# Storing the cumulative sums by chunk, joining small transfers, and starting the SSD and gate loads on GpSimd's queue

## The chip, the cores and the metric

The kernel runs on one core of one Trainium2 chip. Its time is the device time of one execution in microseconds (us). Before the change it is 2260.72 us (median of 3 runs, 2260.71 to 2261.99). A profiled execution is a run of its own: its own time was 2257.6 us, and its trace spans 2255.6 us from the first to the last instruction.

Engines are named as in the profile: PE is the matrix engine (TensorE), DVE is VectorE, ACT is ScalarE, POOL is GpSimd, SP is SyncE. SP does no arithmetic here; it starts transfers.

## The reference

One decoder layer in FP32, with 1024 tokens and a width of 1024. Cut to what matters here:

```python
h = rms_norm(x, norm_mix_g)
z, xbc, dt_raw, q_a, kv_a, k_rope, gates = split(h @ w_in)
# Mamba-2: y_t = sum_{s<=t} (C_t.B_s) exp(sum_{s<k<=t} a_k) x_s dt_s, in chunks of 128 tokens
#   a_cum = cumsum(dt * A) in each chunk; 4 groups of 8 heads
y_ssd = rms_norm_by_group((ssd(silu(conv4(xbc)), dt, a_cum) + d_skip*xs) * silu(z)) @ w_ssd_proj
y_mla = causal_attention(q, k, v) @ w_mla_proj          # 16 heads
g_ssd, g_mla = split(sigmoid(gates + gate_b))
x = x + (g_ssd * y_ssd + g_mla * y_mla) @ w_o
u_gate, u_val = split(conv3(rms_norm(x, norm_ffn_g) @ w_up))
x = x + (silu(u_gate) * u_val) @ w_down                 # d_ff 2816
```

## The kernel before

**Arithmetic.** Every FP32 product is made of three reduced-precision products. A matrix is split into a high part (`whi`, an ACT copy, L152) and a low part (`wlo`, a subtraction, L153), and `mm3` adds hi·hi, hi·lo and lo·hi (L174, L175, L176). The subtraction for weights runs on POOL until L1102 and on DVE after it (`w_eng`). A weight piece of 512 columns is loaded into `wraw`, which has two buffers, so one load runs while the piece before it is split; `whi` and `wlo` are double-buffered too.

**Stages.** (1) The first norm and the small projections, to about 118 us. (2) Attention, to about 700 us, with tiles of z and of the gates computed in its background. (3) The state-space part (SSD), 700 to about 1290 us: four groups g of eight heads, eight chunks of 128 tokens in each. In its background run the convolutions and z tiles of the next group and, in group 3, the output projection of attention (`mla_tiles`, from about 1140 us). (4) The merge, 1303 to 1570 us, in two halves of 512 tokens: for each 128 output channels `ct` a product with `w_ssd_proj`, then gate and sum, then the product with `w_o` and the residual x. (5) The gated MLP.

**What passes through DRAM.** The cumulative sums `ac_d` ([32 heads, 1024 tokens]), z (`z_d`), the gates (`g_d`), the attention output (`at_d`) with its denominators (`l_d`), SSD's output (`y_d`), the gated attention part (`m_d`) and the new residual (`x2_d`, called `x_d` in the profile) are stored and loaded again.

- In each SSD chunk, `abc_load` (L788) reads the chunk's 8 x 128 sums and repeats them on all 128 partitions, 512 KB, and `z_load` (L796) reads the chunk's z, 256 KB. Both are started by ACT. `abc` has three buffers, and the MLA tiles and loads borrow them in group 3; `zt` has two.
- In `mla_tiles`, `one` (L1028) loads the gate of one tile, 256 KB, on SP, placed directly behind the SP instruction ahead of it in program order, and stores the product in `m_d` (L1035).
- In the merge, the gate `gt` (L1213) and the attention part `mt` (L1215) of each `ct` are started by ACT, 16 of each. DVE makes `gt` times the product (L1223) and adds `mt` (L1224). The first weights of the MLP, `ur` (L1126, L1127), are four loads of 512 KB, started by SP in the second half's first steps of the program text.
- The residual x is loaded at L1237 in four transfers of 512 KB per half, and the sum of half 0 is stored in `x2_d` in four transfers of 512 KB (L1276), each before one norm. That norm (`norm`, L233 to L254) overwrites the same tile in place, so its last instruction (L254) waits for the store. The sum of half 1 is stored in 16 transfers of 128 KB on ACT (L1270).

**Order.** PE's order is written out: a chain of dependences (L1563 on) keeps its instructions in program order. On the other engines a scheduler sets the order when the program is built. Each engine and each queue then works strictly in that order, so an instruction that waits holds back all behind it on its engine. Where `behind(name)` stands, the instruction just written is tied behind another one.

## Time and profile before

| what | value |
|---|---|
| median of 3 runs | 2260.72 us |
| profiled execution, its own time | 2257.6 us |
| span of its trace | 2255.6 us |
| PE busy | 2184.2 us (97%) |
| DVE busy | 1433.8 us (64%) |
| ACT busy | 1010.7 us (45%) |
| POOL busy | 758.7 us (34%) |
| packets on SP's queue (q1) | 101232, 214.73 MB |
| packets on ACT's queue (q10) | 57520, 36.84 MB |

How it is read: a time of the trace is counted from its first instruction. "Waits" are groups of idle times, each with the engine that waited, its line, and what came last. A window gives the busy time of each engine, the TensorE clock that was granted, the mean busy share of the 16 DMA engines and what they moved. The share of the DMA engines is the time their packets took, which depends on the packets' size as well as on the bytes.

### The profile page before, as it was taken

To read this page: it belongs to the slowest core of one execution; us is meant where nothing else is said; L and a number is where in the kernel's file an instruction comes from. 1 tells how busy PE (TensorE), PEld (TensorE's weight loads), DVE (VectorE), ACT (ScalarE), POOL (GpSimd) and SP (SyncE) were. 2 spreads that over 40 slices of the span, in tenths; PEclk is the share of its full clock that TensorE was granted. 3 is DMA by queue.
4 is the path that set the end of the run, shared out by engine and by line. 5 is a ranking of instruction groups with operands and counts; after the bars stand their busy time and mean duration, and the time that the engine had idled before them with its cause. 6 is when DMAs were issued, how large, how long until landed. Compare 5 with 4: busy or idle time off the path is not lost.

```text
span 2255.6 us, 31367 instructions
## 1 busy us (share of the span) xinstructions
PE 2184.2 (97%) x11488; PEld 1771.6 (79%) x11488; DVE 1433.8 (64%) x2496; ACT 1010.7 (45%) x1852; POOL 758.7 (34%) x799
## 2 busy tenths in 40 slices
PE   8999999999999999999989999999899999999999
PEld 7877777777777887777877778989778888888887
DVE  4567665667662469897966845546887767774432
ACT  5444454454443446555644424325544444443231
POOL 2244433444232235464523300003365555510000
PEclk9999999999999999999999999999999999999999
DMA  4121111111114235654367556453122222237541
GB/s 144 58 67 49 49 43 53 54 53 38 53 49 121 67 89 143 174 153 153 107 176 218 181 198 227 159 168 113 56 94 79 80 84 78 81 124 259 198 138 66
DMA packets 158905, 253.56 MB, mean 112 GB/s; under 512 B 13504, under 2 KB 68480, under 8 KB 158752
## 3 DMA queue, kind: packets, MB, share of 16 engines
q1 hardware_dynamic: 101232, 214.73, 28.2%
q10 hardware_dynamic: 57520, 36.84, 6.9%
q8 instruction: 90, 1.47, 0.3%
q14 instruction: 63, 0.52, 0.1%
HBM read 194.63 MB, written 56.89 MB: 112 GB/s over the span
## 4 chain that ended last, share of the span: by engine, by line
PE 70%; DVE 16%; DMA 5%; ACT 4%; issue 2%; POOL 1%; SPq 0%; ACTq 0%; DVEq 0%; POOLq 0%
PE lin L174 11%; PE lin L176 11%; PE lin L175 11%; PE dps L174 8%; PE dps L176 8%; PE dps L175 8%; PE pv L669 2%; DMA rb<-at_d 2%; PE s L174 1%; DVE xg L812 1%; PE s L175 1%; PE s L176 1%; PE s L626 1%; DMA wraw<-in_w_mla 1%; DVE qk L587 1%
## 5 line engine op out<-in xcount | busy, mean ns | idle before, releaser
L174 PE MATMUL lin<-h,whi 128*128 128x512 f32 x1440 | 595.4, 413 | 10.8 <-DVE lt L329 7.9
L176 PE MATMUL lin<-h,wlo 128*128 128x512 f32 x1440 | 567.4, 394 | 9.4 <-DVE wlo L153 8.2
L175 PE MATMUL lin<-h,whi 128*128 128x512 f32 x1440 | 565.8, 393 | 0.0
L174 PEld LDWEIGHTS lin<-h,whi 128*128 128x128 f32 x1440 | 273.1, 190 | 94.2 <-issue 33.7
L176 PEld LDWEIGHTS lin<-h,wlo 128*128 128x128 f32 x1440 | 272.5, 189 | 71.3 <-DVE wlo L153 9.0
L175 PEld LDWEIGHTS lin<-h,whi 128*128 128x128 f32 x1440 | 273.6, 190 | 53.3 <-issue 6.7
L152 ACT CAST whi<-wraw 128x512 fp32r<-128x512 f32 x276 | 165.2, 618 | 268.8 <-PE lin L175 110.9
L153 POOL TENSOR_TENSOR wlo<-wraw,whi 128x512 fp32r<-128x512 f32 x134 | 196.1, 1481 | 232.7 <-ACT whi L152 215.8
L658 ACT ACTIVATE e<-s 128x512 f32<-128x512 f32 (+1 forms) x192 | 93.7, 492 | 166.0 <-DVE s L656 141.3
L663 POOL TENSOR_TENSOR acc<-acc,e 128x512 f32<-128x512 f32 (+3 forms) x80 | 79.6, 994 | 232.5 <-ACT e L658 219.0
L153 DVE TENSOR_TENSOR wlo<-wraw,whi 128x512 fp32r<-128x512 f32 x142 | 99.8, 721 | 87.1 <-ACT whi L152 86.8
L153 DVE TENSOR_TENSOR h<-ar,h 128x1024 fp32r<-128x1024 f32 x40 | 48.9, 1225 | 109.3 <-ACT h L152 109.1
L152 ACT CAST h<-ar 128x1024 fp32r<-128x1024 f32 x40 | 42.2, 1054 | 125.8 <-PE lin L175 115.0
L175 PE MATMUL dps<-wlo,h 128*128 128x512 f32 x240 | 93.4, 389 | 0.0
L174 PE MATMUL dps<-whi,h 128*128 128x512 f32 x240 | 93.4, 389 | 0.0
L176 PE MATMUL dps<-whi,h 128*128 128x512 f32 x240 | 93.4, 389 | 0.0
L850 ACT ACTIVATE seg<-abc,acum 128x128 f32<-128x128 f32 x256 | 82.0, 391 | 24.8 <-PE yp L891 16.7
L812 DVE SCALAR_TENSOR_TENSOR xg<-craw,cl,xg 128x1024 f32<-128x1024 f32 x48 | 75.9, 1580 | 18.2 <-ACT xg L810 17.8
L1191 POOL TENSOR_TENSOR h<-x,h 128x512 fp32r<-128x512 f32 x8 | 11.1, 1389 | 220.9 <-ACT h L1190 220.9
L663 DVE TENSOR_TENSOR acc<-acc,e 128x512 f32<-128x512 f32 (+3 forms) x80 | 53.5, 669 | 41.3 <-ACT e L658 40.7
L1138 ACT CAST xhi<-ur 128x512 fp32r<-128x512 f32 (+1 forms) x41 | 34.1, 831 | 88.9 <-PE dps L175 80.0
L669 PE MATMUL pv<-e,vt 128*64 128x512 f32 (+3 forms) x384 | 72.9, 498 | 0.0
(581 smaller groups left out, 5179.5 us busy)
## 6 DMA issues: line engine op xcount, KB each, us to landing
wraw<-in_w_main SPq DMA_DIRECT2D x112, 256.0 KB
ur<-in_w_up SPq DMA_DIRECT2D x44, 512.0 KB
ar<-a_d SPq DMA_DIRECT2D x40, 512.0 KB
abc<-ac_d ACTq DMA_DIRECT2D x32, 512.0 KB
wraw<-in_w_ssd SPq DMA_DIRECT2D x64, 256.0 KB
wraw<-in_w_down SPq DMA_DIRECT2D x44, 256.0 KB
a_d<-uc SPq DMA_DIRECT2D x22, 512.0 KB
g_d<-lt SPq DMA_DIRECT2D x32, 256.0 KB
```

The lines of the kernel that those rows point to most:

```text
L152: S.copy(hi, raw)
L153: (eng or V).tensor_sub(lo, raw, hi.bitcast(F32))
L174: PE.matmul(ps, lhsT=ah, rhs=bh, start=first, stop=False, **more)
L175: PE.matmul(ps, lhsT=ah, rhs=bl, start=False, stop=False, **more)
L176: PE.matmul(ps, lhsT=al, rhs=bh, start=False, stop=last, **more)
L587: V.tensor_tensor(qk[:, :, 2 + hd, 0:64], qk[:, :, 2 + hd, 0:64], rr[:, :, 2 + hd:3 + hd].broadcast_to([P, 4, 64]), op=ALU.mult)
L658: S.activation(e[:, c0:512], ps[:, 0:w], AF.Exp)
L663: (V if hd else G).tensor_tensor(accs[hd][:, c0:512], accs[hd][:, c0:512], e[:, c0:512], op=ALU.add)
L669: PE.matmul(pv[hd * 64:(hd + 1) * 64, c0:512], lhsT=vt[:, j, hd * 64:(hd + 1) * 64], rhs=es[hd][:, c0:512], start=first, stop=last)
L812: V.scalar_tensor_tensor(c, raw[:, k:k + T], col(cw + k), c, op0=ALU.mult, op1=ALU.add)
L850: S.activation(seg[:, hd, :], abc[:, hd, :], AF.Relu, bias=acum[:, c, 8 * g + hd:8 * g + hd + 1], scale=-1.0)
L1138: S.copy(hi, r)
```

## The change

```diff
-    ac_d = dram.tile([HEADS, T], F32, name="ac_d")
+    ac_d = dram.tile([NT, HEADS, P], F32, name="ac_d")
-    l_d = dram.tile([MH, T], F32, name="l_d")
+    l_d = dram.tile([4 * MH, 256], F32, name="l_d")
...
-    nc.sync.dma_start(out=ac_d, in_=act_)
+    nc.sync.dma_start(out=ac_d.rearrange("c h t -> h c t"), in_=act_.rearrange("h (c t) -> h c t", t=P))
...
-            for c in range(4):
-                a = half * 512 + (c % 2) * 256
-                nc.sync.dma_start(out=l_d[2 * pr + c // 2, a:a + 256], in_=lr[32 * c:32 * c + 1, 0:256])
+            r0 = 4 * (2 * pr + half)
+            nc.sync.dma_start(out=l_d[r0:r0 + 4, :], in_=lr[0:128:32, 0:256])
...
-                nc.scalar.dma_start(out=t, in_=ac_d[8 * g:8 * g + 8, c * P:(c + 1) * P].partition_broadcast(P))
+                nc.gpsimd.dma_start(out=t, in_=ac_d[c, 8 * g:8 * g + 8, :].partition_broadcast(P))
...
-                nc.scalar.dma_start(out=t, in_=z_d[4 * g * P:4 * (g + 1) * P, c * P:(c + 1) * P]
+                nc.gpsimd.dma_start(out=t, in_=z_d[4 * g * P:4 * (g + 1) * P, c * P:(c + 1) * P]
...
-                        name = last(mybir.EngineType.SP)
-                        nc.sync.dma_start(out=gt, in_=g_d[(8 + ct) * P:(9 + ct) * P, s])
-                        behind(name)
+                        nc.gpsimd.dma_start(out=gt, in_=g_d[(8 + ct) * P:(9 + ct) * P, s])
...
-    def w_raw(q):
+    def w_raw(q, name=None):
...
-        nc.sync.dma_start(out=q.r1, in_=w_up[q.j])
-        nc.sync.dma_start(out=q.r2, in_=w_up[FFT + q.j])
+        for raw, j in ((q.r1, q.j), (q.r2, FFT + q.j)):
+            nc.sync.dma_start(out=raw, in_=w_up[j])
+            if name:
+                behind(name)
...
-                    w_raw(q0)
-                    w_raw(q1)
+                    w_raw(q0, loaded)
+                    w_raw(q1, loaded)
...
-                    nc.scalar.dma_start(out=gt, in_=g_d[ct * P:(ct + 1) * P, s])
+                    nc.gpsimd.dma_start(out=gt, in_=g_d[ct * P:(ct + 1) * P, s])
-                    nc.scalar.dma_start(out=mt, in_=m_d[ct * P:(ct + 1) * P, s])
+                    nc.gpsimd.dma_start(out=mt, in_=m_d[ct * P:(ct + 1) * P, s])
...
-                for i in range(4):
-                    r0 = (half * 4 + i) * P
-                    nc.sync.dma_start(out=big[:, i, :], in_=x[r0:r0 + P, :])
-                    behind(loaded)
+                nc.sync.dma_start(out=big, in_=x[s, :].rearrange("(i p) c -> p i c", p=P))
+                behind(loaded)
...
-                                if half:
-                                    nc.scalar.dma_start(out=x2_d[512 + i * P:512 + (i + 1) * P, qs], in_=big[:, i, qs])
+                                if half and i == 3:
+                                    nc.scalar.dma_start(out=x2_d[s, qs].rearrange("(i p) c -> p i c", p=P),
+                                                        in_=big[:, :, qs])
...
-                    for i in range(4):
-                        nc.sync.dma_start(out=x2_d[i * P:(i + 1) * P, :], in_=big[:, i, :])
+                    nc.sync.dma_start(out=x2_d[s, :].rearrange("(i p) c -> p i c", p=P), in_=big)
```

`loaded` is the last weight load of step ct = 5 of the merge's half. The x load of each half stands behind it, before and after; in the changed program the `ur` loads stand behind that of half 0. The reads of `l_d` (L991 and L1066 before) follow its new shape. Counted over the program: SP starts 710 transfers instead of 783, ACT has 112 instructions fewer, and POOL has 112 more: 32 loads of `abc`, 32 of `zt`, 16 gates of `mla_tiles`, and 32 of `gt` and `mt`. PE's order is the same. Lines of the changed kernel are numbered one or two higher from L88 on.

Where the change moves instructions, three places matter below. The first is POOL in the SSD stage, one chunk, before (its `sq` stands at 959.7 us in the trace): `st` is the decay of the carried state, `sq` and `sqs` sum squares for the group norm, `rb` scales an attention tile, `wlo` are low parts of weights.

```order
L879 TENSOR_TENSOR st<-st,cdec 128x512 [waits DVE_49,PE_49]
L915 TENSOR_TENSOR sq__9571<-sq__9571 128x256 [waits Activation_49]
L916 TENSOR_TENSOR sqs<-sq__9571 128x128 [waits Pool_49]
L981 TENSOR_TENSOR rb<-rb,nb 128x512 [waits DMAHW6_49,DMAHW4_49,DMAHW3_49]
L153 TENSOR_TENSOR wlo<-wraw,whi 128x512 [waits DMAHW0_49,PE_49,Activation_49]
L153 TENSOR_TENSOR wlo<-wraw,whi 128x512 [waits DMAHW1_49,Activation_49]
```

The same place in the changed program:

```order
L879 TENSOR_TENSOR st<-st,cdec 128x512 [waits DVE_49,PE_49]
L788 DMA abc<-ac_d 128x1024 [waits DMASW3_49]
L796 DMA zt<-z_d 128x4x128 [waits DMASW4_49,DMASW0_49,DVE_49]
L915 TENSOR_TENSOR sq__9787<-sq__9787 128x256 [waits Activation_49]
L916 TENSOR_TENSOR sqs<-sq__9787 128x128 [waits Pool_49]
L981 TENSOR_TENSOR rb<-rb,nb 128x512 [waits DMAHW3_49,DMAHW5_49,DMAHW2_49,DMAHW1_49]
L154 TENSOR_TENSOR wlo<-wraw,whi 128x512 [waits DMAHW0_49,PE_49,Activation_49]
L154 TENSOR_TENSOR wlo<-wraw,whi 128x512 [waits DMAHW2_49,Activation_49]
```

The two loads now stand between the state decay and the group norm, ahead of the low parts.

The second place is POOL in group 3 of the changed program, with the gate loads of `mla_tiles` (L1029 there) among the low parts of its weights:

```order
L796 DMA zt<-z_d 128x4x128 [waits DMAHW1_49,DMASW6_49,DMAHW3_49,DMASW5_49,DVE_49]
L916 TENSOR_TENSOR sqs<-sq__11378 128x128 [waits Pool_49]
L1029 DMA rb<-g_d 128x512 [waits DMAHW4_49,DVE_49]
L154 TENSOR_TENSOR wlo<-wraw,whi 128x512 [waits PE_49,Activation_49]
L788 DMA abc<-ac_d 128x1024 [waits PE_49]
L154 TENSOR_TENSOR wlo<-wraw,whi 128x512 [waits DMAHW2_49,Activation_49]
L1029 DMA rb<-g_d 128x512 [waits DMAHW2_49,DMASW0_49,DVE_49]
```

Before, the gate loads and their waits stood on SP, the sums' and z's on ACT.

The third place is DVE at the end of half 0 of the merge. Before, with the four stores of the new residual (`x_13408` is its tile, L254 the norm that overwrites it):

```order
L1266 TENSOR_TENSOR x_13408<-dps,x_13408 128x256 [waits PE_49]
L248 SCALAR_TENSOR_TENSOR nst<-nst 128x1 [waits DVE_49]
L254 TENSOR_SCALAR x_13408<-x_13408,nst 128x1024 [waits DMAHW0_49]
L153 TENSOR_TENSOR wlo<-wraw,whi 128x512 [waits DMAHW6_49,Activation_49]
L153 TENSOR_TENSOR wlo<-wraw,whi 128x512 [waits DMAHW7_49,Activation_49]
```

And in the changed program, with one store:

```order
L154 TENSOR_TENSOR wlo<-wraw,whi 128x512 [waits DMAHW0_49,Activation_49]
L255 TENSOR_SCALAR x_13360<-x_13360,nst 128x1024 [waits DMAHW1_49]
L255 TENSOR_SCALAR x_13360<-x_13360,nst 128x1024 [waits DVE_49]
L234 TENSOR_REDUCE nst<-sq_13362 128x1 [waits DVE_49] x2
L154 TENSOR_TENSOR wlo<-wraw,whi 128x512 [waits DMAHW2_49,PE_49,Activation_49]
L242 TENSOR_SCALAR nst<-nst 128x1 [waits DVE_49] x2
L154 TENSOR_TENSOR wlo<-wraw,whi 128x512 [waits DMAHW3_49,Activation_49]
```

The norm's wait is now for the only store, and two low parts that the next output tile needs stand behind it.

More of the change, by code (lines that the diff above doesn't have):

```diff
@@ L989, in normalize @@
                 for hd in range(2):
-                    nc.sync.dma_start(out=rb[64 * hd:64 * hd + 64, :], in_=l_d[2 * k + hd, s].partition_broadcast(64))
+                    r0 = 4 * (2 * k + n % 2) + 2 * hd
+                    nc.sync.dma_start(out=rb[64 * hd:64 * hd + 64, :],
+                                      in_=l_d[r0:r0 + 2, :].rearrange("a b -> (a b)").partition_broadcast(64))
                 loaded.append((raw, rb, at_d[k * P:(k + 1) * P, s]))
@@ L1065, in tile_hybrid_layer @@
         ls = dp.tile([P, P], F32, name="bt")
-        lv = l_d.rearrange("h (c t) -> (h c) t", t=P)
+        lv = l_d.rearrange("r (c t) -> (r c) t", t=P)
         for n, _ in enumerate(conv_group(0)):
```

## The prediction

> **What bounds the kernel now.** I read the head of the page first, then PE's waits from 690 to 1620 us, where nearly all edits lie, then windows of 5 us around those waits, and last the chain of work and the queues.
>
> ```profile
> span 2255.6 us, 31367 instructions
> PE 2184.2 (97%) x11488; PEld 1771.6 (79%) x11488; DVE 1433.8 (64%) x2496; ACT 1010.7 (45%) x1852; POOL 758.7 (34%) x799
> ```
>
> PE's own work sets the time, and its order and count do not change. All that any edit can take away is PE's idle time, 2255.6 - 2184.2 = 71.4 us, and matmuls that ran at a lower granted clock. PE's waits in the stages touched:
>
> ```profile
> PE lin L176 <- DVE wlo L153: 8.2, 2, 5.0
> PE lin L174 <- DVE lt L329: 7.9, 2, 4.9
> ...
> PE lin L174 <- ACT whi L152: 2.9, 2, 2.2
> ```
>
> Columns: total us, times, longest. Three places hold the first and the last of these rows and the longest wait of the other. In the windows the columns are length, PE, PEld, DVE, ACT and POOL busy, clock, DMA share, GB/s:
>
> ```profile
> 1155.00:1160.00 5.00, 3.99 (x16) 3.02 (x17) 0.54 (x1) 2.21 (x4) 2.52 (x2) 1.00 0.65 135
> 1160.00:1165.00 5.00, 2.80 (x16) 2.16 (x15) 0.00 (x0) 0.00 (x0) 0.00 (x0) 1.00 0.99 169
> 1165.00:1170.00 5.00, 2.27 (x5) 1.84 (x6) 1.00 (x2) 4.16 (x11) 3.39 (x4) 0.66 0.59 193
> 1170.00:1175.00 5.00, 5.00 (x14) 3.58 (x13) 4.40 (x8) 2.40 (x6) 0.95 (x2) 0.65 0.84 265
> 1185.00:1190.00 5.00, 2.23 (x9) 1.28 (x8) 2.73 (x10) 2.39 (x5) 1.98 (x2) 1.00 0.95 346
> ...
> 1285.00:1290.00 5.00, 4.07 (x22) 3.18 (x21) 4.94 (x9) 4.42 (x9) 1.00 (x2) 1.00 0.58 177
> 1290.00:1295.00 5.00, 2.74 (x8) 2.18 (x9) 4.09 (x16) 0.32 (x2) 0.00 (x0) 0.79 0.72 247
> 1295.00:1300.00 5.00, 5.00 (x25) 4.20 (x24) 1.38 (x2) 1.80 (x3) 0.00 (x0) 0.87 0.33 112
> ...
> 1310.00:1315.00 5.00, 1.45 (x7) 0.87 (x5) 2.57 (x3) 0.23 (x1) 2.00 (x2) 0.84 0.87 334
> 1315.00:1320.00 5.00, 3.54 (x8) 2.82 (x9) 3.70 (x3) 0.77 (x2) 2.54 (x2) 0.50 0.48 150
> ```
>
> Place A (1155 to 1190): idle 1.01 + 2.20 + 2.73 + 2.77 = 8.7 us, and 7.27 us of matmuls at a clock near 0.655, a loss of 2.5: 11.2 us. Place B (1285 to 1300): idle 0.93 + 2.26 = 3.2, clock 2.74 x 0.21 + 5.00 x 0.13 = 1.2: 4.4 us. Place C (1310 to 1320): idle 3.55 + 1.46 = 5.0, clock 1.45 x 0.16 + 3.54 x 0.50 = 2.0: 7.0 us. The clock falls just behind a long idle time, so a stall costs more than its length. Together 22.6 us: the ceiling of what the change can win there.
>
> What ends them is a transfer each time. From the chain of work (start, us, what):
>
> ```profile
> 1156.72 8.76 DMA wraw<-in_w_mla
> ...
> 1176.09 10.64 DMA wraw<-in_w_mla
> ...
> 1280.96 4.84 DMA chan<-g_d
> ...
> 1306.36 8.27 DMA ur<-in_w_up
> ```
>
> **The change, part by part.** *The sums by chunk.* For 890 to 1100 us the queues show packets, MB and share:
>
> ```profile
> q1 hardware_dynamic: 11847, 21.29, 28.8%
> q10 hardware_dynamic: 21976, 11.02, 24.1%
> ```
>
> ACT's queue takes 24.1/11.02 = 2.2% of the engines' time per MB, SP's 28.8/21.29 = 1.35%. The difference is packets of 0.5 KB against 1.8 KB. `abc` is 32 loads of 512 KB, now in runs of 512 B; in the new layout the eight rows of a chunk are one run of 4 KB. Two starts in A, by ACT and by SP:
>
> ```profile
> 1154.74 0.45 ACTq L788 DMA_DIRECT2D abc<-ac_d  x1
> 1159.08 2.40 SPq L1028 DMA_DIRECT2D rb<-g_d  x1
> ```
>
> The `abc` load went out two us ahead of the late weights, and the DMA engines were then 0.99 busy for only 169 GB/s, against 0.95 for 346 GB/s at 1185. So one part of A is packets, and it goes; the other is bytes, and stays. The gate load took SP 2.40 us to start with the engines full; it leaves SP, so the weight loads behind it start earlier. Bounds 0 and 11.2 us; I take 60%, **-6.7 us**, because four of A's five windows have the engines at 0.59 to 0.99 with a rate under 270 GB/s.
>
> *The gates of group 3.* B hangs on `chan<-g_d`, which now starts from POOL, 16 of them. Nothing makes it shorter; it may start earlier or later. Bounds -4.4 and, where POOL waits, the rival below; I take a quarter, **-1.1 us**.
>
> *The first MLP weights.* In C, four `ur` loads (2.1 MB) went out beside the first `gt` and `mt`:
>
> ```profile
> 1305.26 0.34 ACTq L1213 DMA_DIRECT2D gt<-g_d  x1
> 1311.38 0.69 DVE L1223 SCALAR_TENSOR_TENSOR gt<-gt,lin 128x512 f32<-128x512 f32 x1 [7.34 <-DMA ur<-in_w_up]
> 1313.12 1.62 DVE L1224 TENSOR_TENSOR gt<-gt,mt 128x512 f32<-128x512 f32 x1 [1.05 <-DMA mt<-m_d]
> 1314.66 3.43 DVE L153 TENSOR_TENSOR wlo<-wraw,whi 128x512 fp32r<-128x512 f32 x2
> ```
>
> PE stopped 1.45 us into C's first window, at 1311.45, for that `wlo`. At 334 GB/s `ur` took 6.3 of the 8.27 us in the chain. Without it `gt` can start up to 6 us earlier, and the `wlo`, 5 us late, comes in time. The POOL sums of `ur` that ran beside it (2.00 and 2.54 us in C's windows) leave too. I keep back one us for POOL's starts: bounds 0 and -7, taken **-6.0 us**.
>
> *The starts on POOL.* The trace has none. The nearest are ACT's and SP's (min/median/max ns):
>
> ```profile
> L788 ACTq DMA_DIRECT2D abc<-ac_d x32: 366/366/528, 700.3 to 1243.5; - x32
> L1028 SPq DMA_DIRECT2D rb<-g_d x10: 319/426/2737, 1159.1 to 1268.9; - x10
> ```
>
> So 0.37 to 2.74 us each, two per chunk, 0.7 to 5.5 us. A chunk lasts 210/14 = 15 us at 890 to 1100 (14 `abc` loads there), and POOL is busy half of it:
>
> ```profile
> 890.00:1100.00 210.00, 199.95 (x1221) 160.16 (x1222) 181.93 (x266) 121.28 (x233) 104.51 (x75) 1.00 0.53 155
> ...
> L153 POOL TENSOR_TENSOR wlo<-wraw,whi 128x512 fp32r<-128x512 f32 x82 | 128.7, 1587 | 180.4 <-ACT whi L152 168.5 <-PE xp L840 7.5 <-PE yp L896 4.2
> ```
>
> POOL idles 7.5 us per chunk, and the low parts queued behind the loads mostly wait for ACT anyway (168.5 us). Both ends fit in; what does not hide is a start that falls just ahead of a needed `wlo`: **+1 us** (0 to 5). ACT loses 96 starts of 0.34 to 0.37 us, some 34 us; busy 121 of 210 us it sets nothing, 0.
>
> *The x load.* x (2 MB) and the four `ur` loads (2 MB) now stand around two weight pairs at ct = 5. Before, with x alone:
>
> ```profile
> 1355.00:1360.00 5.00, 5.00 (x23) 4.14 (x23) 3.18 (x5) 1.77 (x3) 0.00 (x0) 1.00 0.97 328
> ...
> 1363.10 0.62 ACT L152 CAST whi<-wraw 128x512 fp32r<-128x512 f32 x1 [4.38 <-DMA wraw<-in_w_ssd]
> ```
>
> The engines were full, ACT waited 4.38 us for a weight, and PE lost nothing. Twice the bytes take 4.2 MB at 328 GB/s, 13 us, with weights between them; a pair is loaded one pair ahead: **+1 us** (0 to 4, the wait of ACT).
>
> *The store of half 0.* This is the one new wait that I can place. Before:
>
> ```profile
> 1430.73 4.42 SPq L1276 DMA_DIRECT2D x_d<-x  x4
> 1434.92 0.75 DVE L254 TENSOR_SCALAR x<-x,nst 128x1024 f32<-128x1024 f32 x1
> ...
> 1441.88 1.29 DVE L153 TENSOR_TENSOR wlo<-wraw,whi 128x512 fp32r<-128x512 f32 x2
> 1444.94 0.69 DVE L1223 SCALAR_TENSOR_TENSOR gt<-gt,lin 128x512 f32<-128x512 f32 x1 [1.77 <-PE lin L176]
> ...
> 1435.00:1440.00 5.00, 5.00 (x24) 4.14 (x23) 5.00 (x31) 0.92 (x3) 0.00 (x0) 1.00 0.91 325
> ```
>
> Four stores went out as their rows were ready, and each norm waited for its own. Now one store starts after the last sum, near 1435, and the first norm waits for all 2 MB: 6.5 us at 325 GB/s, so until 1442 to 1444. Two norms of 0.75 and the pair of `wlo` follow, the latter from 1444 to 1446; PE needs the first of them near 1444.9, where the product that DVE's L1223 waited for ends and the next begins. The weights are also queued behind the 2 MB. Bounds 0 and 8 (6 us of stall and 2 of clock, as in C); taken **+2.5 us**.
>
> *The stores of half 1* end with one of 512 KB instead of 128 KB, ahead of the last norm, which the MLP's first products need: 0.4 MB more at 325 GB/s is 1.2 us. Taken **+1 us** (0 to 2). *The denominators*: 48 fewer starts on SP during attention, at the 0.43 us of L1028's median 21 us of SP's time; SP does no arithmetic and the transfers were 1 KB each: 0, or a gain.
>
> Sum: -6.7 - 1.1 - 6.0 + 1 + 1 + 2.5 + 1 = **-8.3 us**. The profiled execution took 2257.6, so 2249.3 on its scale; the median lies 3.1 above it, and the forecast is **2252.4 us**.
>
> **The rivals.** *(1) POOL becomes the gate: slower.* POOL works in order, and in group 3 the gate loads stand among the `wlo` of the same stage. Their buffers come free by stores; SP waited for them:
>
> ```profile
> SPq L1028 <- DMA m_d<-rb: 5.8, 1, 5.8
> SPq L1028 <- DMA m_d<-chan: 5.2, 1, 5.2
> ```
>
> On SP such a wait held back loads that had a pair in hand; on POOL it holds back `wlo` itself. ACT's wait of 4.38 us for a weight did not reach PE; a POOL wait longer than that does. If half of the 16 gates lose 2 us so, that is +16 on top of the -8.3: 2268. For it: the two engines already disturb each other, as DVE's pair of `wlo` took 3.43 us beside POOL's sums in C and 1.29 us at 1441.88, and DVE is busy 182 of 210 us at 890 to 1100. Against it: POOL's idle time. A page makes it likelier: the Trainium skill, SBUF — State Buffer (section "SBUF: two separate sides"), says that a load started by GpSimd has its descriptors written by GpSimd and starves while VectorE holds their shared port; by that rule the loads themselves are late wherever DVE is dense. No run here shows a load from POOL yet.
>
> *(2) Only the bytes count: no change.* If A and B are set by bytes and by SP's order, only C goes: -6.0 + 5.5 = -0.5, 2260. For it: the engines moved 346 GB/s at 1185 and PE idled 2.77 us nevertheless. Against it: 0.99 busy at 169 GB/s. The Trainium skill, DMA: Bandwidth & Descriptors (section "Issuing engines are not separate DMA queues"), has it that moving a start to another engine saves only that engine's time; by that rule the move alone gives nothing, and the gain is in packets and in C.
>
> *(3) All three places go* and the store hides: -22.6 + 2 = -20.6, 2240. For it: every one of them ends with a transfer. Against it: B's gate is no smaller.
>
> **How the numbers follow.** A change under 0.2% (4.5 us) cannot be told from none. Chances: the forecast (2247 to 2256) 0.43; rival 3 and what lies between, 0.14; rival 2 0.19; rival 1 0.24. Faster 0.57, same 0.19, slower 0.24. The range goes from rival 3's end, 2240, to just short of rival 1's price, 2266, leaving about one in ten on either side; the forecast's own range is 2247 to 2256.
>
> **What would show it.** Right: no stall of PE over 2 us at 1155 to 1190 and at 1311; `abc` in 4 KB packets, so some 28,000 packets fewer; a wait of DVE's norm for the store near 1435 of 6 us or more, with a PE stall near 1445. Wrong: new PE waits for POOL's `wlo` or `st` between 700 and 1300 (rival 1); A unchanged with the engines full (rival 2); no wait at the norm, which would free another 2.5 us.

## The result and the profile after

The changed kernel takes **2226.32 us** (median of 4 runs, 2224.44 to 2228.39), beside 2261.35 us for the kernel before (4 runs, 2260.71 to 2262.07). The ratio is 0.9845, with a 95% interval of 0.9828 to 0.9862: 35 us faster. The forecast was 2252.4 us and its range ended at 2240, so the direction was right and the size was not: four times the gain, outside the range.

The head of the page of the changed kernel, its packets, and PE's four largest waits from 690 to 1590 us (total us, times, longest):

```profile
span 2222.6 us, 31323 instructions
PE 2173.7 (98%) x11488; PEld 1765.2 (79%) x11488; DVE 1430.4 (64%) x2496; ACT 1012.4 (46%) x1852; POOL 822.4 (37%) x911
...
DMA packets 112714, 253.57 MB, mean 114 GB/s; under 512 B 13168, under 2 KB 19248, under 8 KB 112560
```

```profile
PE sn L874 <- DVE bt L863: 5.1, 3, 3.1
PE dps L175 <- DVE ug L1443: 2.0, 1, 2.0
PE dps L177 <- DVE wlo L1141: 1.2, 1, 1.2
PE np__12753 L955 <- DVE grr L125: 0.8, 1, 0.8
```

The span fell by 33.0 us. PE's idle time went from 71.4 to 2222.6 - 2173.7 = 48.9 us, and PE's own busy time fell by 10.5 us with the same 11,488 matmuls, since fewer of them ran at a lowered clock behind a stall. None of the three waits with which the prediction began (`lin` for `wlo`, `lt` and `whi`) is left in that stretch.

**Where the time came from.** PE runs the same matmuls in the same order in all kernels here. So each matmul of one trace can be paired with its twin in the other, and the difference of their starts, read at the borders of the stages, says where time was gained. The borders are in the time of the kernel before; us gained in each stretch (a minus is lost):

| kernel | to 690 | 690–860 | 860–1100 | 1100–1250 (A) | 1250–1302 (B) | 1302–1330 (C) | rest |
|---|---|---|---|---|---|---|---|
| changed | 0.0 | 4.9 | 8.8 | 8.2 | 4.7 | 7.1 | -0.3 |
| changed, again | 0.4 | 4.9 | 8.8 | 8.4 | 5.1 | 7.1 | 0.4 |
| new layout alone | 0.8 | 4.9 | 4.4 | 10.9 | -0.6 | 0.2 | -1.1 |
| `abc`, z from POOL alone | 0.4 | -1.2 | -13.1 | 3.4 | 2.0 | 2.2 | -2.6 |
| `ur` moved alone | 1.2 | -1.2 | -2.7 | -1.3 | -0.4 | 5.4 | -3.8 |
| changed, old queues | 0.3 | 4.9 | 4.4 | 12.3 | -0.9 | 6.7 | 0.6 |
| changed, old queues, again | 3.9 | 4.9 | 2.8 | 12.1 | 0.4 | 6.7 | -0.4 |
| changed, gates on SP | 0.7 | 4.9 | 8.8 | 11.6 | 2.9 | 7.1 | -1.7 |
| changed, `abc`, z from ACT | 0.7 | 4.9 | 4.4 | 8.8 | 4.9 | 6.2 | -4.4 |
| changed, pieces as before | 0.1 | 4.9 | 8.9 | 7.1 | 4.3 | 7.1 | -3.6 |
| changed, late `wlo` | 2.2 | 4.9 | 8.8 | 9.7 | 1.4 | 7.1 | -1.3 |
| old queues, early `wlo` | 0.9 | 4.9 | 4.4 | 12.4 | 2.8 | 6.1 | 1.2 |

Each row is one profiled execution against one execution of the kernel before. How far such numbers carry is seen in the `ur` row, where up to 2.7 us are lost in stretches that this kernel doesn't touch, and in the two rows of the old queues, one kernel traced twice, which differ by 3.6 us before 690, 1.6 at 860–1100 and 1.3 at B. So a difference of 4 us counts, and a smaller one where several rows repeat it or a wait stands beside it.

The prediction knew of A, B and C, 22.6 us at most. Two fifths of the gain, 4.9 + 8.8 = 13.7 us, came from 690 to 1100, where it expected none.

**What the prediction didn't see.** In the kernel before, just before 718 us and from 920 on, ACT stands still, and what ends its wait is a transfer that its next instruction doesn't read. From the timeline of the kernel before (start, us, engine, line, out<-in, and in brackets the idle time ahead with what ended it), then from its chain of waits in that stretch:

```profile
928.26 0.37 ACTq L796 DMA_DIRECT2D zt<-z_d  x1
928.67 1.06 ACT L852 ACTIVATE seg<-seg 128x1024 f32<-128x1024 f32 x1 [8.18 <-DMA rb<-at_d]
929.63 1.04 ACT L866 ACTIVATE abc<-abc 128x1024 f32<-128x1024 f32 x1
930.71 1.23 DVE L867 TENSOR_TENSOR abc<-abc,chan 128x1024 f32<-128x1024 f32 x1 [7.56 <-ACT abc L866]
```

```profile
915.07 3.15 DMA at_d<-rb
918.23 0.02 issue
918.24 9.99 DMA rb<-at_d
928.24 0.02 issue
928.26 0.37 ACTq L796
```

L852 reads `seg` and writes `seg`; it has nothing to do with `rb`, the attention output that SP loads. What waits is the z load that stands ahead of it on ACT. The instructions of ACT at this place, with the semaphores that each waits for:

```
L850 ACTIVATE seg<-abc,acum 128x128
L796 DMA zt<-z_d 128x4x128 [waits DMAHW6_49]
L852 ACTIVATE seg<-seg 128x1024 [waits Activation_49]
L866 ACTIVATE abc<-abc 128x1024
```

`DMAHW6` is one of a few completion counters that transfers from SP and from ACT share in this program: the z load may not start before the transfer that used this counter last, here SP's load of `rb`, has landed. 41 of ACT's 64 starts of `abc` and z wait for such a counter, some of them for an earlier load into the same buffer. The load of `rb` took 9.99 us for 256 KB beside an `abc` load in 512-byte packets, ACT's exponentials (L852, L866) stood 8.18 us behind the start, and DVE stood 7.56 us behind ACT. PE's product `sn` then waits three times for `bt`, which DVE copies late: 0.94 us at 936.6, 1.45 at 951.8 and 1.53 at 967.0. PE has five more waits from 885 to 1030, 0.7 to 1.7 us each (at 891.4, 906.8, 907.9, 1008.6 and 1024.3), and ahead of those ACT waits for no transfer; experiments 5 and 6 come back to them. In the changed kernel the same starts wait on POOL, for counters of POOL's own transfers and for DVE (total us, times, longest):

```profile
POOL wlo L154 <- ACT whi L153: 129.3, 30, 9.1
POOL zt L796 <- DVE xg L905: 75.2, 19, 8.2
...
POOL chan L1029 <- DMA m_d<-chan: 6.2, 2, 5.0
```

75 us of POOL's time go by in L796's waits for `xg` alone, and no wait for POOL stands among PE's.

The stall of that kind at 718 us, just behind attention, in windows of 5 us (length, PE, PEld, DVE, ACT, POOL busy, clock, DMA share, GB/s), of the kernel before and of the changed one:

```profile
710.00:715.00 5.00, 5.00 (x24) 4.14 (x23) 0.00 (x0) 2.23 (x8) 0.00 (x0) 1.00 0.96 199
715.00:720.00 5.00, 1.98 (x8) 1.34 (x7) 0.69 (x1) 2.07 (x5) 0.00 (x0) 0.95 0.72 255
720.00:725.00 5.00, 5.00 (x17) 3.94 (x17) 0.69 (x1) 4.97 (x12) 1.04 (x1) 0.71 0.47 124
```

```profile
710.00:715.00 5.00, 5.00 (x24) 4.14 (x23) 0.55 (x1) 4.74 (x12) 1.53 (x2) 1.00 0.89 291
715.00:720.00 5.00, 5.00 (x24) 4.14 (x23) 0.83 (x2) 2.83 (x5) 2.54 (x2) 1.00 0.32 106
```

Engines 0.96 busy for 199 GB/s before, 0.89 for 291 after; PE loses 3.0 us and then runs at a clock of 0.71 before, nothing after.

### The profile page after: what moved, and what is told of

It is laid out like the page before. It is cut to its first block, busy times and chain, and to the rows that moved or that the text cites. A ratio compares the mean times of both kernels' runs of the same rounds, so it can differ in the third digit from the quotient of the medians.

```text
span 2222.6 us, 31323 instructions
## 1 busy us (share of the span) xinstructions
PE 2173.7 (98%) x11488; PEld 1765.2 (79%) x11488; DVE 1430.4 (64%) x2496; ACT 1012.4 (46%) x1852; POOL 822.4 (37%) x911
## 4 chain that ended last, share of the span: by engine, by line
PE 75%; DVE 13%; ACT 4%; DMA 3%; issue 2%; POOL 1%; SPq 0%; DVEq 0%; ACTq 0%; POOLq 0%
PE lin L175 12%; PE lin L177 12%; PE lin L176 12%; PE dps L177 8%; PE dps L175 8%; PE dps L176 8%; PE pv L670 2%; PE s L175 2%; PE s L176 1%; PE s L177 1%; PE s L627 1%; PE yp L891 1%; PE sn L874 1%; DMA wraw<-in_w_ssd 1%; DVE qk L588 1%
## 5 line engine op out<-in xcount | busy, mean ns | idle before, releaser
L175 PEld LDWEIGHTS lin<-h,whi 128*128 128x128 f32 x1440 | 271.4, 188 | 81.6 <-issue 33.4
L175 PE MATMUL s<-qh,kh 97*128 97x512 f32 (+1 forms) x192 | 68.5, 357 | 2.0 <-ACT qh L644 1.1
```

Source lines behind the costliest of these rows:

```text
L175: PE.matmul(ps, lhsT=ah, rhs=bh, start=first, stop=False, **more)
```

## The experiments

Three theories went in. **P (packets):** the gain is the new layout of `ac_d`, whose loads hold up all other transfers no longer. **Q (queues):** the gain is that ACT no longer carries the starts. **O (order):** with starts on POOL the scheduler puts other engines' work, DVE's above all, in another order. Beside them stand the single edits at C, at the joined transfers and at B.

**1. The new layout alone.** The kernel before, with `ac_d` by chunk; ACT still starts everything, and no engine's order changes.

```diff
-    ac_d = dram.tile([HEADS, T], F32, name="ac_d")
+    ac_d = dram.tile([NT, HEADS, P], F32, name="ac_d")
-                nc.scalar.dma_start(out=t, in_=ac_d[8 * g:8 * g + 8, c * P:(c + 1) * P].partition_broadcast(P))
+                nc.scalar.dma_start(out=t, in_=ac_d[c, 8 * g:8 * g + 8, :].partition_broadcast(P))
```

> The kernel before with the sums stored by chunk and nothing else; every engine keeps its order. Three theories on where the 35 us went. Theory P (packets: 512 B rows made the weights late): the stalls at 718 us, at 1155 to 1190 and at 1290 go, most of the SSD stage's gain too, 2235 to 2243 us. Theory Q (queues: ACT and SP are relieved of starts): within 4 us of before, 2257 to 2261. Theory O (order: the scheduler puts VectorE's SSD work in another order once GpSimd starts the loads): the stalls at 718 and 1155 may shrink, the SSD stage at 890 to 1030 gains under 2 us, 2246 to 2254.

Measured: 2238.88 us beside 2259.02, ratio 0.9913 (0.9898 to 0.9928), 20 us faster. The queue's row for 890 to 1100 us and ACT's wait:

```profile
q10 hardware_dynamic: 9936, 11.27, 18.7%
```

```profile
ACT seg L852 <- DMA rb<-at_d: 6.2, 2, 3.9
```

The share per MB fell from 2.19% to 1.66%. The wait behind the z load is still there but half as long: 6.2 us in place of 13.6, the longest 3.9 in place of 8.2. The layout gives all of the 4.9 us at 718, half of the 8.8 at 860–1100, and more than all of A. The half at 860–1100 is the three waits of PE behind that stall of ACT: they are gone, though ACT still waits 3.9 us. P missed the stall near 1290, which stayed (B, -0.6), and O expected less than the 4.4 us.

**2. The starts alone.** The kernel before, with `abc` and z started by POOL and the old layout.

```diff
-                nc.scalar.dma_start(out=t, in_=ac_d[8 * g:8 * g + 8, c * P:(c + 1) * P].partition_broadcast(P))
+                nc.gpsimd.dma_start(out=t, in_=ac_d[8 * g:8 * g + 8, c * P:(c + 1) * P].partition_broadcast(P))
-                nc.scalar.dma_start(out=t, in_=z_d[4 * g * P:4 * (g + 1) * P, c * P:(c + 1) * P]
+                nc.gpsimd.dma_start(out=t, in_=z_d[4 * g * P:4 * (g + 1) * P, c * P:(c + 1) * P]
```

> The kernel before with the loads of sums and z in the SSD chunks started by GpSimd, in the old layout with 512 B rows. Theory P: no better than before, 2257 to 2265, since the packets stay. Theory Q: 2236 to 2246. Theory O: the SSD stage at 890 to 1030 gains its 9 us, the stalls at 1155 to 1190 stay: 2250 to 2254. The old layout needs 1024 descriptors per load from GpSimd, so a start may cost more than the 0.58 us of the new layout.

Measured: 2263.32 us, ratio 1.0022 (1.0009 to 1.0035): slower, if by little. Its starts on POOL (ns, min/median/max), PE's first wait, and the window in which it lost most:

```profile
L788 POOL DMA_DIRECT2D abc<-ac_d x32: 884/942/1104, 700.1 to 1255.3; - x32
```

```profile
PE lin L174 <- DVE lt L329: 17.0, 5, 7.0
```

```profile
920.00:925.00 5.00, 2.84 (x11) 1.99 (x11) 3.29 (x6) 0.00 (x0) 0.00 (x0) 1.00 1.07 174
925.00:930.00 5.00, 1.08 (x5) 0.56 (x3) 0.00 (x0) 0.00 (x0) 0.00 (x0) 1.00 0.70 212
```

The engines were full at 174 GB/s, DVE ran out of work within the first window, ACT and POOL had none, and PE waited for `lt`: the core waited for bytes. The -13.1 us at 860–1100 are a sum: PE gains 8.5 us at the waits of that stretch, as O expected (3.9 at the three behind ACT's stall, 4.6 at 891, 907 and 1024), and loses 13.6 here and 7.9 between 1030 and 1050 of the old time. Why the 512-byte loads stop it at these two places isn't shown. So the starts alone don't make the gain; whether they add to the new layout is asked by experiment 6.

**3. The first MLP weights alone.** The kernel before, with the `ur` loads tied behind the x loads.

```diff
-                    w_raw(q0)
-                    w_raw(q1)
+                    w_raw(q0, loaded)
+                    w_raw(q1, loaded)
```

> The kernel before with the first MLP weights ordered behind the load of step 5 and nothing else. All theories: the stall at 1316 us goes (7 us of idle time and clock), 2253 to 2256 us. If the stall stays, the late gate was not the transfers beside it.

Measured: 2252.47 us, ratio 0.9973 (0.9961 to 0.9986), 6.5 us faster. The window where PE had stopped for 3.55 us:

```profile
1310.00:1315.00 5.00, 5.00 (x24) 4.14 (x23) 0.13 (x1) 1.14 (x2) 0.00 (x0) 1.00 0.85 253
```

**4. All sizes and layouts, old queues.** The changed kernel with every start that went to POOL back on ACT or SP.

```diff
-                nc.gpsimd.dma_start(out=t, in_=ac_d[c, 8 * g:8 * g + 8, :].partition_broadcast(P))
+                nc.scalar.dma_start(out=t, in_=ac_d[c, 8 * g:8 * g + 8, :].partition_broadcast(P))
...
-                        nc.gpsimd.dma_start(out=gt, in_=g_d[(8 + ct) * P:(9 + ct) * P, s])
+                        name = last(mybir.EngineType.SP)
+                        nc.sync.dma_start(out=gt, in_=g_d[(8 + ct) * P:(9 + ct) * P, s])
+                        behind(name)
```

> The changed kernel with every load that GpSimd started given back to ScalarE (sums, z, gt, mt) or SyncE (gates of group 3). Theory P: most of the gain stays, 2226 to 2234 us. Theory Q: 2246 to 2254. Theory O: 2234 to 2242, with the SSD stage's 9 us gone.

Measured: 2230.07 us, ratio 0.9876 (0.9862 to 0.9891); once more, on the chip of experiment 9 and as its measure:

> The changed layout and sizes with every start on its old queue, once more, as the measure for the run with the earlier weight on the same chip: 2229 to 2231 us by both theories, a ratio of 0.987 to 0.988, with the PE stall on wlo near 1269 us.

2230.28 us, ratio 0.9878 (0.986 to 0.9896). So 26 to 29 of the 35 us come without any start on POOL. Against the changed kernel the two rows of the table lack 4.4 and 6.0 us at 860–1100 and 5.6 and 4.3 at B, and have 4 more in A. The sum of single edits says the same: 20.1 (layout) + 6.5 (`ur`) = 26.6 us.

**5 and 6. The changed kernel again, and with `abc` and z back on ACT.** The two ran on the same chip; the second differs from the first by these two starts.

```diff
-                nc.gpsimd.dma_start(out=t, in_=ac_d[c, 8 * g:8 * g + 8, :].partition_broadcast(P))
+                nc.scalar.dma_start(out=t, in_=ac_d[c, 8 * g:8 * g + 8, :].partition_broadcast(P))
-                nc.gpsimd.dma_start(out=t, in_=z_d[4 * g * P:4 * (g + 1) * P, c * P:(c + 1) * P]
+                nc.scalar.dma_start(out=t, in_=z_d[4 * g * P:4 * (g + 1) * P, c * P:(c + 1) * P]
```

> The changed kernel itself, beside the three variants below on the same chip: 2222 to 2229 us, about 6 us below the variant with all starts on the old queues (2230), if the queues are worth anything in the new layout.

> The changed kernel with the loads of sums and z started by ScalarE again, in the new layout. Theory L (a start that waits in ScalarE's order for an earlier transfer's semaphore lane holds back the arithmetic behind it): ScalarE's waits for rb<-at_d ahead of seg come back, 3 to 4 us each, and the SSD stage from 885 to 1015 us loses 2 to 4 us: 2 to 5 us slower than the changed kernel. Theory N (the starts cost nothing once packets are large): same within 1.5 us, and no ScalarE wait for a transfer that its next instruction doesn't read.

Measured: 2223.64 us (2222.79 to 2225.61) for the changed kernel, ratio 0.9851 (0.9832 to 0.987), and 2231.18 us (2229.19 to 2232.24), ratio 0.988 (0.9864 to 0.9896), with the starts on ACT: 7.5 us apart, and the runs don't overlap. ACT's wait is back:

```profile
ACT seg L852 <- DMA rb<-at_d: 5.5, 2, 3.3
```

With the new layout, moving these 64 starts is worth 7.5 us by the medians, while with the old one it cost 4. But theory L has the place wrong. ACT's wait of 3.3 us stands at 917 us, and at the three waits of PE behind it this kernel gains 4.5 us on the kernel before, no less than the changed kernel with its 4.0. The 4.4 us that it lacks at 860–1100 are lost at 891, 907 and 1024 of the old time, where ACT waits for no transfer; every traced kernel with `abc` and z started by POOL gains 4.6 to 4.7 us there, and none with the starts on ACT gains anything. DVE's order there is another one, too. With the starts on ACT, as in the kernel before, the product `abc` (L867) of this chunk stands behind the copy `bt` (first two lines, PE waits 1.5 us for it at 885.8); in the changed kernel it stands ahead (last two lines, and PE doesn't wait):

```profile
885.49 0.28 DVE L863 COPY bt<-sp 128x128 f32<-128x128 f32 x1
886.82 1.22 DVE L867 TENSOR_TENSOR abc<-abc,chan 128x1024 f32<-128x1024 f32 x1
```

```profile
878.41 1.21 DVE L867 TENSOR_TENSOR abc<-abc,chan 128x1024 f32<-128x1024 f32 x1
884.62 0.28 DVE L863 COPY bt<-sp 128x128 f32<-128x128 f32 x1
```

So theory O may hold here. No run pins this order, so it isn't shown whether the order, the time of the starts on ACT, or both make the 4.4 us.

Of the rest, 3.6 us stand between 1390 and 1400 of the old time, where no `abc` or z is loaded any more. PE waits there for ACT's `m`, and its clock falls to 0.81 and 0.85:

```profile
1367.57 0.39 PE L175 MATMUL dps<-whi,m 128*128 128x256 f32 x1 [1.34 <-ACT m L1229]
```

This place loses 4.1 us here and 0.5 in the changed kernel of this experiment. In the ten traces of kernels with moved `ur` loads it loses 0 to 4.1 us, in those of experiments 1 and 2, without that move, nothing. So it goes with the `ur` loads, and its share of the 7.5 us can't be put down to the 64 starts.

**7. The gates back on SP.** The changed kernel, with only `mla_tiles`' gate loads on SP as before.

```diff
-                        nc.gpsimd.dma_start(out=gt, in_=g_d[(8 + ct) * P:(9 + ct) * P, s])
+                        name = last(mybir.EngineType.SP)
+                        nc.sync.dma_start(out=gt, in_=g_d[(8 + ct) * P:(9 + ct) * P, s])
+                        behind(name)
```

> The changed kernel with the 16 gate loads of group 3 started by SyncE again. If the stall near 1267 us (1290 before) went because the gates left SyncE, it comes back: 4 to 6 us slower than the changed kernel. If packets alone removed it, the time is the same within 2 us. The alignment of the first runs says the former: with packets alone (first run) the stall stayed.

Measured: 2225.17 us (2223.5 to 2227.54), ratio 0.9855 (0.9838 to 0.9872), the same as the changed kernel. The stall on `wlo` at B did not come back, so the gates' queue is not what freed B; that theory fell. (B gains only 2.9 us here because PE then waits 2.6 us for the group norm's `grr`.) This is the stall in the kernel before:

```profile
1292.26 0.50 PE L176 MATMUL lin<-h,wlo 128*128 128x512 f32 x1 [3.18 <-DVE wlo L153]
```

The engines' orders gave the next theory. In the kernel before, VectorE's two `wlo` splits of the first SSD output weight stand behind all `h` splits of the y tiles; in the changed kernel and in this one the scheduler has put them between those splits. No line of the diff asks for that. Moving starts to POOL changed what the scheduler saw, and with it DVE's order.

**8. B by order alone: the splits late.** The changed kernel, all starts where the change put them, with these two splits tied behind the last y split, as they stood before the change.

```diff
         (eng or V).tensor_sub(lo, raw, hi.bitcast(F32))
+        if pin[0]:
+            behind(pin[0])
...
             ya0[11] = ordered_split(staged.pop(0))
+            tail.append(last(mybir.EngineType.DVE))
...
-            ws = [load_w(w_ssd[0, kp], [P, KD, P]) for kp in range(2)]
+            pin[0] = tail[0]
+            ws = [load_w(w_ssd[0, 0], [P, KD, P])]
+            pin[0] = None
+            ws.append(load_w(w_ssd[0, 1], [P, KD, P]))
```

> The changed kernel with one edit: the two VectorE splits of the first SSD output weight (w_ssd[0, 0], its low halves) are tied behind the split of the last y tile, so that they stand in VectorE's order where they stood before the change, behind the h splits. Every DMA start stays where the change put it. Theory O (the 4 to 5 us that the change gained near 1290 us of the old run come from VectorE's order alone, which the scheduler changed when the starts moved): the PE stall on wlo returns at 1260 to 1275 us, 3 to 6 us long, and the time is about 5 us above the changed kernel's, 2227 to 2232 us, a ratio to the kernel before of 0.985 to 0.988. Rival T (the gain comes from the transfers: the weights or the gates arrive earlier): the pinned order costs at most 1 us, 2223 to 2226 us, and no stall over 2 us is there.

Measured: 2228.42 us (2224.97 to 2230.18) beside 2256.63, ratio 0.9866 (0.9851 to 0.9882). PE's stall is back, at the place where the changed kernel has none:

```profile
1265.26 0.50 PE L182 MATMUL lin<-h,wlo 128*128 128x512 f32 x1 [2.38 <-DVE wlo L155]
```

```profile
1265.00:1270.00 5.00, 4.74 (x14) 3.78 (x15) 3.13 (x13) 1.24 (x2) 0.00 (x0) 0.66 0.42 138
```

Its 2.4 us are just under the 3 to 6 expected, and the clock of 0.66 in the window behind adds to them; B's share in the table falls from 4.7 to 1.4 us. No run of the changed kernel stands beside it on this chip, and its interval overlaps that of the changed kernel elsewhere, so the whole time can't tell the theories apart; the stall can.

**9. B by order alone: the splits early, with the old queues.** The kernel of experiment 4, with the load of this weight written four steps earlier and its last split tied in place. The load keeps its place in SP's order; ACT's cast of the weight's second half moves ahead with DVE's splits.

```diff
             def y_step(j):
+                if j == 28:
+                    name = last(mybir.EngineType.DVE)
+                    early.append(load_w(w_ssd[0, 0], [P, KD, P]))
+                    behind(name)
...
-            ws = [load_w(w_ssd[0, kp], [P, KD, P]) for kp in range(2)]
+            ws = [early[0], load_w(w_ssd[0, 1], [P, KD, P])]
```

> The changed layout and sizes with every start back on its old queue (as in the experiment with the old queues, 2230 us), and one edit: the load of w_ssd[0, 0] is written four steps earlier, so that its VectorE splits stand ahead of the last h splits. Theory O (order alone): the stall near 1269 us shrinks from about 5 us to under 2, and the time falls by 3 to 5 us to 2225 to 2227 us, without any start moved. Rival T (transfers): the splits wait for the weights instead, the time stays at 2229 to 2231 us.

Measured: 2227.38 us (2225.05 to 2230.95), ratio 0.9869 (0.9852 to 0.9886), beside 2230.28 for the same kernel without the edit. The first row is PE's wait in the kernel of experiment 4, the second PE's longest wait in B with the edit:

```profile
PE lin L177 <- DVE wlo L154: 3.0, 1, 3.0
```

```profile
PE np__12753 L957 <- DVE grr L126: 2.1, 1, 2.1
```

The stall on `wlo` is gone without any start moved. B wins 2.4 us against the second trace of experiment 4's kernel (0.4 to 2.8), 3.7 against the first (-0.9 to 2.8), and 2 more go to the next wait in line, for the group norm's `grr`. Medians that are 2.9 us apart with overlapping ranges prove little; the rows show the cause.

**10. The joined transfers.** The changed kernel with x loaded and the sums stored in the pieces of before (512 KB in four, 128 KB in sixteen).

```diff
-                nc.sync.dma_start(out=big, in_=x[s, :].rearrange("(i p) c -> p i c", p=P))
-                behind(loaded)
+                for i in range(4):
+                    r0 = (half * 4 + i) * P
+                    nc.sync.dma_start(out=big[:, i, :], in_=x[r0:r0 + P, :])
+                    behind(loaded)
...
-                    nc.sync.dma_start(out=x2_d[s, :].rearrange("(i p) c -> p i c", p=P), in_=big)
+                    for i in range(4):
+                        nc.sync.dma_start(out=x2_d[i * P:(i + 1) * P, :], in_=big[:, i, :])
```

> The changed kernel with the loads and stores of the residual in their old pieces (four of 512 KB, sixteen of 128 KB). By the prediction's terms the joined transfers cost 2.5 + 1 us at the stores and part of 1 at the load, so this would be 3 to 4 us faster than the changed kernel. By the trace of the changed kernel, where the norm waits 5.7 us and the matrix engine nothing, it is the same within 2 us, and only VectorE's 5.7 us wait goes.

Measured: 2228.12 us (2 runs, 2227.58 and 2228.66), ratio 0.9867 (0.9844 to 0.9891), beside 2223.64 for the changed kernel on the same chip. The prediction charged the joined transfers 1 + 2.5 + 1 = 4.5 us; taking them apart makes the kernel not faster but, in these two runs, 4.5 us slower. Of that some 2 us stand at the end of half 1, where PE waits for the last norm:

```profile
PE dps L1180 <- DVE x L255: 1.2, 1, 1.2
```

The kernels with these pieces (before and experiments 1, 2, 3 and 10) wait 0.5 to 1.4 us there, the others at most 0.5. So joining the stores of half 1 saves up to some 2 us. What makes the rest of the 4.5 us is open; the first four runs of the changed kernel (2224.44 to 2228.39) overlap with these two. None of these kernels beats the changed one by more than the runs can tell.

## Why the prediction was wrong, step by step

**The ceiling: wrong, and the step that failed.** "Together 22.6 us: the ceiling of what the change can win there." It was built from the three places of the longest waits, and left out 690 to 1100 us, where the change won 13.7 us. The row `lin <- lt` that was quoted has two waits, 7.9 us with a longest of 4.9; the second, 3.0 us at 719, is not in A, B or C. And the third row of that list stands behind the prediction's three dots; none of its waits is longer than 1.7 us:

```profile
PE sn L874 <- DVE bt L863: 7.1, 5, 1.7
```

With three more for `seg` and `abc` these small waits make up PE's idle time from 885 to 1030, 145.00 - 134.86 = 10.1 us before and 2.2 after. They had more than one cause: the layout took the three behind ACT's stall, the moved starts four others (experiments 1 and 6), and one stays:

```profile
885.00:1030.00 145.00, 134.86 (x855) 107.32 (x852) 129.27 (x188) 79.86 (x154) 73.35 (x54) 1.00 0.57 160
```

```profile
885.00:1030.00 145.00, 142.82 (x878) 114.68 (x879) 131.78 (x192) 86.90 (x165) 95.08 (x81) 1.00 0.54 182
```

**"ACT loses 96 starts … busy 121 of 210 us it sets nothing, 0": wrong.** The busy share of ACT was taken for its effect. Moving the 64 starts of `abc` and z in the new layout is worth 7.5 us by the medians, 4.4 of them at 860–1100. It is not the wait that the row `ACT seg <- DMA rb<-at_d` shows (13.6 us in two waits): the layout alone halved that wait and gave PE back all that it had lost behind it. With the moved starts comes another order on DVE, which the prediction didn't consider; the cause of the 4.4 us stays open between the order and the starts. (By the traces ACT starts 7 transfers instead of 115, 108 fewer and not 112, and SP 708 instead of 781.)

**The sums by chunk, -6.7 us: right in mechanism, a third of its size.** 60% of A was taken because "one part of A is packets, … the other is bytes, and stays". Alone the layout gives 20.1 us by the medians; the pairing has 4.9 at 718, 4.4 at 860–1100 and 10.9 in A, nearly A's whole 11.2. In the changed kernel A wins 8.2: its gains add to 12.2, and 4.1 is given back at 1173 of the old time in a new wait of `sn` for `bt`:

```profile
1152.95 1.75 PE L874 MATMUL sn<-xde,bt 128*128 128x512 f32 x2 [3.07 <-DVE bt L863]
```

The "28,000 packets fewer" were right: in experiment 1, where ACT still starts everything, its queue has 28,848 packets instead of 57,520, 28,672 fewer. The changed kernel's 46,191 fewer can't be compared: see the last section.

**The gates of group 3, -1.1 us: wrong in its cause.** B won 4.7 us. The gates' queue has no part in it (experiment 7); DVE's order has (8 and 9). That the scheduler answers moved starts with another order on an engine that has no line in the diff is a step that the prediction doesn't have. Two opposite edits show the cause; that it makes all of B's 4.7 us isn't shown, they account for 3.3 (late) and 2.4 to 3.7 (early).

**The first MLP weights, -6.0 us: right.** 6.5 us alone, 7.1 in the changed kernel at C, whose whole ceiling was 7.0.

**The starts on POOL, +1 us: durations inside the bounds, the cost 0.** The bounds were 0.37 to 2.74 us each; measured (ns, min/median/max):

```profile
L788 POOL DMA_DIRECT2D abc<-ac_d x32: 531/577/736, 700.0 to 1223.0; - x32
L796 POOL DMA_DIRECT2D zt<-z_d x32: 754/767/820, 700.7 to 1240.2; - x32
```

POOL's busy time rose by 63.7 us, and PE has no wait for POOL.

**The x load, +1 (0 to 4): right.** Behind the `ur` and x loads ACT waits for other loads, and between 1390 and 1400 of the old time the changed kernel loses 1.4 us in one trace and 0.5 in the other; kernels with the same move lose 0 to 4.1 (experiment 6). **The stores of half 1, +1: 0, and rather a gain.** No kernel with joined stores loses time at the end of half 1, and the old pieces lose up to 2.4 us there (experiment 10).

**The store of half 0, +2.5: the wait came as described, the stall did not.** The one store goes out at 1402.99, and the norm waits:

```profile
1410.49 1.42 DVE L255 TENSOR_SCALAR x<-x,nst 128x1024 f32<-128x1024 f32 x2 [5.68 <-DMA x_d<-x]
1411.24 1.21 ACT L153 CAST whi<-wraw 128x512 fp32r<-128x512 f32 x2 [7.15 <-DMA wraw<-in_w_ssd]
1412.05 0.69 DVE L154 TENSOR_TENSOR wlo<-wraw,whi 128x512 fp32r<-128x512 f32 x1
...
1413.38 0.68 DVE L1225 SCALAR_TENSOR_TENSOR gt<-gt,lin 128x512 f32<-128x512 f32 x1
```

```profile
1405.00:1410.00 5.00, 5.00 (x24) 4.14 (x23) 0.00 (x0) 0.00 (x0) 0.00 (x0) 1.00 0.98 331
```

DVE, ACT and POOL do nothing for 5 us, and PE is busy throughout. The `wlo` is done at 1412.74, the product before it ends by 1413.38: a margin of about 0.6 us. The prediction put both within a microsecond of each other and took a third of the upper bound; the lower one, 0, was it. With so small a margin, that the lower one came is luck as much as judgment.

**The rivals.** Rival 3 (2240) came nearest, since it let A, B and C all go (22.6 us; they made 20.0), yet it shared the ceiling. Rival 1, POOL as the gate, fell: there is a wait of 5.0 us for `m_d<-chan` on POOL as it described, but no wait of PE for POOL. The Trainium skill, SBUF — State Buffer (section "SBUF: two separate sides"), by which a load started by GpSimd starves while VectorE holds the port that they share, would have made the loads late. In the new layout `abc` lands after 5.2 us (median) from POOL and 4.7 from ACT, z after 3.4 from POOL and 4.8 from ACT, and PE has no wait for either. How long VectorE held that port no run here shows. The rows of `abc`:

```profile
abc<-ac_d POOLq DMA_DIRECT2D x32, 512.0 KB, 5.2
```

```profile
abc<-ac_d ACTq DMA_DIRECT2D x32, 512.0 KB, 4.7
```

Rival 2, only bytes count, fell on the layout. Its rule from the Trainium skill, DMA: Bandwidth & Descriptors (section "Issuing engines are not separate DMA queues"), that moving a start saves only the engine's time, would have the move give next to nothing. By the medians it cost 4 us in the old layout (experiment 2) and gained 7.5 in the new one (experiments 5 and 6): with the move PE stopped for `lt` at new places in the old layout, and in both layouts it gained at 891, 907 and 1024.

**The sum.** The pairing gives 33.4 us against the 8.3 forecast: 13.7 at 690–1100 that had no term, 1.5 more in A, 3.6 in B, 1.1 in C, and 5.5 of costs of which 0.3 show in the rest.

## What to carry to other kernels

Look in the waits for an instruction whose releaser is a transfer that it doesn't read: a start ahead of it in its engine's order is waiting, and the work behind the start waits with it, whatever the engine's busy share. Then look whether the bounding engine waits behind it: here 8.2 us of ACT cost PE three waits, and the 3.3 us left after the new layout cost it none. Shrink the packets' number first and move the start then; here the move alone cost 4 us and on top of the smaller packet count it gained 7.5. After any edit that moves work between queues, compare the scheduled order on every engine, also on those without a line in the diff, before giving a gain to the edit.

## What the runs showed of the hardware

- **A broadcast in 512-byte runs fills the DMA engines.** They were 1.07 busy for 174 GB/s (experiment 2) and 0.96 for 199 (before, 710 to 715); with 4 KB runs 1.03 for 390 GB/s:

```profile
705.00:710.00 5.00, 5.00 (x24) 4.14 (x23) 0.69 (x1) 3.72 (x11) 1.54 (x2) 1.00 1.03 390
```

  The `abc` load started by POOL lands after 9.8 us in the old layout and 5.2 in the new one.
- **The cost of a start on POOL depends on the load's shape**, where on ACT it hardly does: 0.94 us for `abc` in 512-byte runs, 0.58 in 4 KB runs, 0.77 for z (half the bytes, in 512-byte runs), 0.54 for a gate, against 0.33 to 0.37 on ACT for all.
- **Packets of POOL's queue aren't comparable with those of the others.** The old `abc` and z are 50,176 packets on ACT's queue (57,520 less the 7,344 that stay) and 7,168 on POOL's for the same 25.17 MB (experiment 2):

```profile
q0 software_dynamic: 7168, 25.17, 7.1%
q10 hardware_dynamic: 7344, 11.67, 1.5%
```
- **Most stalls of PE were followed by a lowered clock**, 0.50 to 0.89 in the windows behind those of 2.4 us and more for `wlo` and `lt`; behind the waits for `grr`, 2.6 us in experiment 7 and 2.1 in experiment 9, it stayed at 1.00. The 10.5 us by which PE's busy time fell are nearly a third of the span's gain.
